# A relu-mean kernel on Trainium2: one store of the results at the end, or two, the larger of them queued behind the loads

## The chip, the cores and the metric

The kernel runs on one core of one Trainium2 chip. The metric is the device time of one execution in microseconds (us). The kernel before takes 161.66 us (median of 6 runs, 161.41 to 161.91). Two executions of the same kernel thus differ by up to 0.5 us.

## The reference

```python
x = np.random.randn(32, 512, 1024).astype(np.float32)      # 67.1 MB
relu_x = np.maximum(x, 0)
return np.mean(relu_x, axis=-1).astype(np.float32)          # (32, 512), 64 KB
```

There are 16384 rows of 1024 numbers, and each gives one result.

## The kernel before

Each of the 128 partitions holds 128 consecutive rows of x, so it makes 128 consecutive results, 512 B of the output. All loads are issued from SP (SyncE) on one queue: seven times 16 rows a partition (the first cut into 1 and 15), then pieces of 8, 4, 2 and 1 rows, and then the last row in three pieces of columns. ACT (ScalarE) and DVE (VectorE) take rows in turn, POOL (GpSimd) scales the sums, and DVE makes the last result (the line called L181 in the profile, the `scalar_tensor_tensor`).

```python
    finish(full, 0, j0)                 # POOL: results 0 to 111 (j0 = 112)
    ...
    finish(i, j0, j0 + lo)              # POOL: results 112 to 125
    ...                                 # POOL: result 126, from two halves, then_inc(pool, 1)
    dve_row(nc, last[:, 512:768], last[:, D + 1:D + 2]).then_inc(dve, 1)
    nc.vector.wait_ge(act, n_done + 1)
    nc.vector.wait_ge(dve, n_done + 1)
    nc.vector.wait_ge(loaded[i + 3], 16)
    nc.vector.scalar_tensor_tensor(     # DVE: result 127
        out=last[:, 768:], in0=last[:, 768:], scalar=0.0, in1=scale[:, :], op0=ALU.max, op1=ALU.mult,
        accum_out=res[:, J - 1:J],
    ).then_inc(dve, 1)

    nc.sync.wait_ge(pool, 2)
    nc.sync.wait_ge(dve, n_done + 2)
    nc.sync.dma_start(out=outr, in_=res[:, :]).then_inc(stored, 16)
    ...
    nc.sync.wait_ge(stored, 16).then_inc(stored, -16)
```

## Time and profile before

| what | value |
|---|---|
| time, median of 6 | 161.66 us |
| span in the profile | 160.3 us |
| DVE, ACT busy | 46%, 43% |
| DMA | 419 GB/s, packets took 97.8% of the span of the 16 transfer engines |
| last load byte, end of the last result, end of the span | 157.55, 158.66, 160.32 us |

The span is 1.3 to 1.4 us shorter than the time. The profile's lines are shown in the prediction. A transfer *lands* when the last of its 16 semaphore writes has arrived (a semaphore is a counter that another engine waits for); *confirmation* is the stretch from the last of these writes' own record to the end of the span. The text below calls *tail* the stretch from the end of the last result (the end of L181's read of the accumulator) to the end of the span: 160.32 - 158.66 = 1.65 us here, by the unrounded figures.

### The profile page before, as it was taken

How to read it: one execution, taken by the hardware profiler on the slowest of the kernel's cores; microseconds unless marked ns; L12 is line 12 of the kernel's file. 1: busy time of each engine (PE TensorE's matmuls, PEld its weight loads, DVE VectorE, ACT ScalarE, POOL GpSimd, SP SyncE). 2: the span in 40 equal slices, each digit the busy share in tenths (PEclk: the TensorE clock that was granted, in tenths of full speed). 3: DMA queues.
4: the chain of work that ended last, by engine and by line, in shares of the span. 5: the costliest groups of instructions: out<-in, count | busy, mean ns of one | idle time of the engine just before them, and what ended most of it. 6: DMA issues, size and time to landing. Idle time of an engine off the chain costs nothing. (4 is left out here: it accounts for less than half of the span.)

```text
span 160.3 us, 344 instructions
## 1 busy us (share of the span) xinstructions
DVE 74.3 (46%) x132; ACT 69.3 (43%) x131; POOL 1.3 (1%) x8
## 2 busy tenths in 40 slices
DVE  0000059700795008940099301991039900498994
ACT  0000059800793008930099101990039700496974
POOL 1000000000000000000000000000000000000001
DMA  9988996996989989979969969969969969999993
GB/s 376 491 383 353 491 523 262 523 523 262 523 360 425 523 360 425 523 327 458 523 294 491 523 278 507 523 262 523 523 262 523 523 262 523 392 392 405 417 404 99
DMA packets 2304, 67.18 MB, mean 419 GB/s; under 512 B 256, under 2 KB 640, under 8 KB 1024
## 3 DMA queue, kind: packets, MB, share of 16 engines
q1 hardware_dynamic: 2304, 67.18, 97.8%
HBM read 67.11 MB, written 0.07 MB: 419 GB/s over the span
## 5 line engine op out<-in xcount | busy, mean ns | idle before, releaser
L20 DVE TENSOR_SCALAR_CACHE_REDUCE rows<-rows 128x1024 f32<-128x1024 f32 x64 | 73.4, 1208 | 84.0 <-DMA rows<-in_x_dram 83.8
L15 ACT ACTIVATE rows<-rows 128x1024 f32<-128x1024 f32 x64 | 66.2, 1036 | 67.0 <-DMA rows<-in_x_dram 66.8
L15 ACT ACTIVATION_READ_ACCUMULATOR rows<-rows 128x1 f32 x64 | 12.0, 187 | 0.0
L15 ACT ACT_TABLE_LOAD x1 | 1.3, 1283 | 21.8 <-DMA rows<-in_x_dram 21.8
L20 DVE DVE_READ_ACCUMULATOR rows<-rows 128x1 f32 x64 | 5.3, 83 | 0.0
L146 POOL TENSOR_SCALAR res<-sums 128x112 f32<-128x112 f32 (+1 forms) x2 | 0.5, 250 | 154.3 <-DVE rows L20 154.3
L15 ACT ACTIVATE last<-last 128x512 f32<-128x512 f32 x1 | 0.6, 629 | 0.0
L20 DVE TENSOR_SCALAR_CACHE_REDUCE last<-last 128x256 f32<-128x256 f32 x1 | 0.4, 420 | 0.3 <-DMA last<-in_x_dram 0.3
L181 DVE SCALAR_TENSOR_TENSOR last<-last,scale 128x258 f32<-128x258 f32 x1 | 0.4, 428 | 0.1
L131 POOL MEMSET scale<- 128x258 f32 x1 | 0.3, 314 | 1.5 <-POOLq L55 1.5
L171 POOL TENSOR_SCALAR res<-part 128x1 f32<-128x1 f32 x1 | 0.3, 264 | 0.6 <-DVE rows L20 0.6
L15 ACT ACTIVATION_READ_ACCUMULATOR last<-last 128x1 f32 x1 | 0.2, 186 | 0.0
L216 POOL MEMSET const-bfloat16-1.0<- 128x1 bf16 x1 | 0.1, 101 | 0.0
L216 POOL MEMSET const-uint8-127<- 128x1 uint8 x1 | 0.1, 101 | 0.0
L216 POOL MEMSET const-float32-0.0<- 128x1 f32 x1 | 0.1, 98 | 0.2 <-issue 0.2
L216 POOL MEMSET const-float32-1.0<- 128x1 f32 x1 | 0.1, 98 | 0.0
L181 DVE DVE_READ_ACCUMULATOR last<-last,scale 128x1 f32 x1 | 0.1, 84 | 0.0
L20 DVE DVE_READ_ACCUMULATOR last<-last 128x1 f32 x1 | 0.1, 83 | 0.0
## 6 DMA issues: line engine op xcount, KB each, us to landing
rows<-in_x_dram SPq DMA_DIRECT2D x1, 7680.0 KB, 21.3
rows<-in_x_dram SPq DMA_DIRECT2D x1, 4096.0 KB, 39.1
rows<-in_x_dram SPq DMA_DIRECT2D x1, 2048.0 KB, 43.6
rows<-in_x_dram SPq DMA_DIRECT2D x2, 512.0 KB, 25.2
rows<-in_x_dram SPq DMA_DIRECT2D x1, 1024.0 KB, 45.7
last<-in_x_dram SPq DMA_DIRECT2D x1, 256.0 KB, 46.7
last<-in_x_dram SPq DMA_DIRECT2D x2, 128.0 KB, 46.5
rows<-in_x_dram SPq DMA_DIRECT2D x6, 48.7
```

The costliest lines, as they stand in the source:

```text
L15: return nc.scalar.activation(out=src, in_=src, func=ACT.Relu, accum_out=acc)
L20: return nc.vector.tensor_scalar(out=src, in0=src, scalar1=0.0, scalar2=init, op0=ALU.max, op1=ALU.add, accum_out=acc,)
L131: nc.gpsimd.memset(scale[:, :], inv).then_inc(pool, 1)
L146: nc.gpsimd.tensor_scalar(out=res[:, lo:hi], in0=sums[:, lo:hi], scalar1=inv, scalar2=0.0, op0=ALU.mult, op1=ALU.add,)
L171: nc.gpsimd.tensor_scalar(out=res[:, J - 2:J - 1], in0=part[:, 0:1], scalar1=part[:, 1:2], scalar2=inv, op0=ALU.add, op1=ALU.mult,).then_i ...
L181: nc.vector.scalar_tensor_tensor(out=last[:, 768:], in0=last[:, 768:], scalar=0.0, in1=scale[:, :], op0=ALU.max, op1=ALU.mult, accum_out=r ...
L216: nc = _bacc.Bacc("TRN2", target_bir_lowering=False, num_devices=1)
```

## The change

112 of the 128 results of a partition are ready at 148 us, 10 us before the last. The change stores these 112 columns in a transfer of their own, queued behind the loads, so that only 16 columns are left for the end.

```diff
             out=res[:, lo:hi], in0=sums[:, lo:hi], scalar1=inv, scalar2=0.0, op0=ALU.mult, op1=ALU.add,
-        )
+        ).then_inc(pool, 1)
 ...
     nc.sync.wait_ge(pool, 2)
+    nc.sync.dma_start(out=outr[:, :j0], in_=res[:, :j0]).then_inc(stored, 16)
     nc.sync.wait_ge(dve, n_done + 2)
-    nc.sync.dma_start(out=outr, in_=res[:, :]).then_inc(stored, 16)
+    nc.sync.wait_ge(pool, 4)
+    nc.sync.dma_start(out=outr[:, j0:], in_=res[:, j0:]).then_inc(stored, 16)
 ...
-    nc.sync.wait_ge(stored, 16).then_inc(stored, -16)
+    nc.sync.wait_ge(stored, 32).then_inc(stored, -32)
```

## The prediction

> **What bounds the kernel now.** I read the page first: the busy shares, then the forty slices.
>
> ```profile
> DVE 74.3 (46%) x132; ACT 69.3 (43%) x131; POOL 1.3 (1%) x8
> ...
> DMA  9988996996989989979969969969969969999993
> GB/s 376 491 383 353 491 523 262 523 523 262 523 360 425 523 360 425 523 327 458 523 294 491 523 278 507 523 262 523 523 262 523 523 262 523 392 392 405 417 404 99
> ...
> HBM read 67.11 MB, written 0.07 MB: 419 GB/s over the span
> ```
>
> No compute engine is busy for half of the span, while the transfer engines are at 90% or so in every slice but the last. 67.11 MB has to come in, and 67.18 MB over 160.3 us is the 419 GB/s shown. So the stream of loads is the bound, and only what lies after it, the tail, can be touched by a change to the store. The queue's own waits and the grouped DMA issues say how the tail is made:
>
> ```profile
> SPq L188 <- DVE last L181: 46.6, 1, 46.6
> SPq L194 <- SPq L194: 1.1, 1, 1.1
> ...
> out_dram<-res SPq DMA_DIRECT2D x1, 64.0 KB, 1.5
> ```
>
> The first line: SP has issued all loads by 112.1 us and then sits 46.6 us for the last instruction on DVE. The second: after the store it waits another 1.1 us for the store's own semaphore. The third: from the start of the issue to landing the one store takes 1.5 us. The timeline of the last microseconds gives the order:
>
> ```profile
> 157.61 0.26 POOL L171 TENSOR_SCALAR res<-part 128x1 f32<-128x1 f32 x1 [0.62 <-DVE rows L20]
> 157.71 0.42 DVE L20 TENSOR_SCALAR_CACHE_REDUCE last<-last 128x256 f32<-128x256 f32 x1 [0.27 <-DMA last<-in_x_dram]
> 157.90 0.19 ACT L15 ACTIVATION_READ_ACCUMULATOR last<-last 128x1 f32 x1
> 158.05 0.08 DVE L20 DVE_READ_ACCUMULATOR last<-last 128x1 f32 x1
> 158.23 0.43 DVE L181 SCALAR_TENSOR_TENSOR last<-last,scale 128x258 f32<-128x258 f32 x1
> 158.58 0.08 DVE L181 DVE_READ_ACCUMULATOR last<-last,scale 128x1 f32 x1
> 158.74 0.35 SPq L189 DMA_DIRECT2D out_dram<-res  x1
> ```
>
> Columns are start, duration, engine and line. The last result exists at 158.66, the store issue starts at 158.74 and takes 0.35 us. A table of stretches splits what follows:
>
> ```profile
> 157.00:157.55 0.55, 0.43 (x2) 0.52 (x3) 0.00 (x0) 1.00 0.46 143
> 157.55:158.74 1.19, 0.86 (x4) 0.54 (x2) 0.26 (x1) 1.00 0.00 0
> 158.74:159.55 0.81, 0.00 (x0) 0.00 (x0) 0.00 (x0) 1.00 0.00 0
> 159.55:159.95 0.40, 0.00 (x0) 0.00 (x0) 0.00 (x0) 1.00 0.57 164
> 159.95:160.30 0.35, 0.00 (x0) 0.00 (x0) 0.00 (x0) 1.00 0.00 0
> ```
>
> The last two columns are the DMA share and GB/s. The loads' last byte moves at about 157.5. The queue is empty until 159.55. The store's bytes move in only 0.40 us, at a share of 0.57, so 0.40 x 0.57 = 0.23 us of work per engine; before them are 0.81 us of issue and start-up, after them 0.35 us of confirmation. Of the 1.5 us of the store, then, only the 0.40 us depends on how many bytes it has.
>
> **What the Trainium skill says.** "DMA: Bandwidth & Descriptors", section "Anatomy of one DMA", splits a transfer into a fixed part, mostly the receipt of the last write, and a part proportional to bytes. It fits that for another issuing path, but the trace agrees in kind: 0.81 + 0.35 us against 0.40 us for 64 KB. "Perfetto Trace Analysis", section "DMA Instruction - HWDGE (DVE, Sync)", says the issue's recorded window ends before the movement, and that the final semaphore write waits for the confirmed write; here 0.35 us of recorded issue and landing 1.15 us after that agree. The first page again, section "Queues, rings and completion order": each engine takes its ring's descriptors in order. So a store issued in mid-stream from the same queue goes behind the loads already there. The trace shows the backlog (loads issued at 110.7 to 111.6 landed 46.4 to 46.7 us later); no store in it shows the order. The section "Specifications" there puts the line-rate minimum at 512 B, with read-modify-write below. The store of before has rows of exactly 128 x 4 = 512 B; the new ones have 448 and 64 B. No run here shows yet what that costs.
>
> **The change, part by part.**
> 1. *Early store.* The POOL multiply for the first 112 columns runs at 147.66 for 0.29 us, thus ends at 147.95 and now signals. With pool at 2 (the fill of the scale tile is 1), SP issues 128 x 448 B = 57 KB at about 148.0, for 0.35 us of SP, which has been waiting since 112. It finds about 157.5 - 148.0 = 9.5 us of loads ahead of it. Its bytes move as each engine runs out of loads, 157.1 to about 157.9, and with 0.35 us of confirmation it lands at about 158.3. That is before SP even issues the second store. On the path: 0.
> 2. *Second store.* It still waits for DVE at 158.66. The fixed parts stay: 0.08 us to the issue, 0.35 us of issue (128 rows as before; the recorded issues of loads, whose sizes differ widely, take 0.33 to 0.44 us, so bytes do not set it), 0.46 us to the first byte, 0.35 us of confirmation. What shrinks is the movement. Each engine still moves 128 / 16 = 8 rows, of 64 B in place of 512 B. From 0.23 us / 8 = about 28 ns a row of 512 B, I estimate 10 to 15 ns for a row of 64 B, as a row has a fixed part; 8 of them are about 0.1 us. So 0.23 - 0.1 = **0.13 us saved**. The rest of the 0.40 us is that engines do not start together, which stays.
> 3. *Extra wait.* Before, the wait for pool came ahead of the wait for DVE and was long satisfied. Now a wait for pool (4, reached near 157.87) comes after the DVE wait, on the path. DVE passes its three waits ahead of L181 in 158.23 - 158.13 = 0.10 us, thus about 0.03 us each: **0.03 us added**, if SP is like DVE.
> 4. *Signals and end wait.* Two more POOL increments and a final wait for 32 in place of 16: POOL is 1% busy, and the end wait is set by the second store. 0.
>
> Sum: -0.13 + 0.03 = **-0.10 us**, 0.06% of the time. 161.68 - 0.10 = 161.58, which I round to **161.6 us**.
>
> **Rivals.**
> *A. Short rows cost more.* If writing 64 B into a 512 B row takes a read first, the second store's movement or confirmation grows. A read and a write more would cost around the 0.35 us that confirmation takes now (an estimate). [...] For it: the skill's threshold. The time would be 161.68 + 0.03 + 0.2 to 0.35 = about 161.9 to 162.1, so slower by 0.1 to 0.2%.
> *B. The early store delays the last loads.* The load of the last columns was issued at about 111.58 and landed 46.4 us later, 157.98. L181 started at 158.23, when ACT (158.09) and DVE (158.13) had been done; I put the load's slack at 0.15 us. Engines that finish their loads early would send the store while late ones still read. The whole store is 0.23 us of work per engine, and ring order puts it behind on each single engine, so at most 0.1 us would show: 161.7. If it were not queued behind but mixed in, the stream itself would lengthen by its 0.2 us: 161.8.
> *C. The bytes were all that counted.* Were the 1.5 us proportional to bytes, an eighth of them would leave 0.2 us and the time would be 160.4. The empty stretches before and after the movement speak against it. Even so it is 0.8%, within 2%.
> *D. Nothing at all.* If the movement's 0.40 us is wholly spread between engines, the gain is 0 and the extra wait costs 0.03: 161.7.
>
> **Range and chances.** The mechanism lies within about -0.15 to +0.4 us. The three runs of before span 161.49 to 161.85, thus 0.36 us, which is more than the expected effect; the stream of loads, where 1% is 1.6 us, can also differ from one chip or session to another. I take 161.2 to 162.0, three quarters of it noise. For 2% the time would have to move 3.2 us; the whole tail after the last load byte is 160.3 - 157.5 = 2.8 us, and the store only 1.5 of it. So faster by over 2% is excluded short of an error in reading (0.01); slower by over 2% would need the early store to block the stream for 3 us (0.01); within 2% is 0.98.
>
> **What would show it right or wrong.** Right: two stores among the issues, the first of 56 KB issued near 148 with some 10 us to landing, the second of 8 KB issued within 0.2 us of L181's end with about 1.4 us to landing; its movement under 0.40 us; loads' last byte still near 157.5; L181 still near 158.2. A second store landing in 1.6 us or more is rival A; a later L181 after a later load is rival B; 0.5 us to landing is rival C. The prediction is wrong outright if the early store is issued well after 148, if the time per load changes, or if the gap between L181 and the second issue grows by more than 0.1 us.

## The result, and the profile after

The changed kernel takes 161.53 us (median of 6 runs, 161.43 to 161.74) against 161.66 us. The ratio is 0.9994 with a 95% interval of 0.9981 to 1.0006, so the two are the same at 2%, and this measurement alone does not tell the difference from none. Ratios here are the mean time of one kernel's fast runs over that of the other's of the same rounds, so they are not quite the ratio of the medians quoted.

The single profiles show what the times cannot. The DMA issues of the changed kernel (KB and us to landing), and the queue's own waits:

```profile
out_dram<-res SPq DMA_DIRECT2D x1, 56.0 KB, 10.2
out_dram<-res SPq DMA_DIRECT2D x1, 8.0 KB, 1.4
...
SPq L189 <- POOL res L146: 35.9, 1, 35.9
SPq L191 <- POOL res L171: 9.5, 1, 9.5
SPq L197 <- SPq L197: 1.0, 1, 1.0
SPq L192 <- DVE last L181: 0.8, 1, 0.8
```

The early store waits 10.2 us in the queue and lands; the late one takes 1.4 us in place of 1.5. The wait for DVE is now put down to L192, the store itself, where before it was L188, a line ahead of the store. That turns out to matter. The timeline's end:

```profile
147.96 0.35 SPq L189 DMA_DIRECT2D out_dram<-res  x1
...
158.01 0.08 DVE L20 DVE_READ_ACCUMULATOR last<-last 128x1 f32 x1
158.18 0.43 DVE L181 SCALAR_TENSOR_TENSOR last<-last,scale 128x258 f32<-128x258 f32 x1
158.54 0.08 DVE L181 DVE_READ_ACCUMULATOR last<-last,scale 128x1 f32 x1
158.65 0.34 SPq L192 DMA_DIRECT2D out_dram<-res  x1
```

The last result exists at 158.62 and the issue starts at 158.65, 0.03 us later; before, it was 0.08 us. The stretches of the tail (the last two columns are the DMA share and GB/s):

```profile
157.70:158.65 0.95, 0.83 (x4) 0.35 (x2) 0.13 (x1) 1.00 0.00 0
158.65:159.48 0.83, 0.00 (x0) 0.00 (x0) 0.00 (x0) 1.00 0.00 0
159.48:159.70 0.22, 0.00 (x0) 0.00 (x0) 0.00 (x0) 1.00 0.42 38
159.70:160.10 0.40, 0.00 (x0) 0.00 (x0) 0.00 (x0) 1.00 0.00 0
```

Issue and start-up are as long as before (0.83 against 0.81 us with these borders), the movement is about half as long (0.22 against 0.40 us), the confirmation is as long. The trace's records of single packets give the same without rounding to borders:

| part of the tail, us | before | after |
|---|---|---|
| end of the last result to start of the issue | 0.08 | 0.03 |
| start of the issue to the first row's start | 0.85 | 0.84 |
| first row's start to the end of the last semaphore write | 0.36 | 0.21 |
| from there to the end of the span | 0.38 | 0.39 |
| sum | 1.65 | 1.47 |
| mean time of one row on its engine, ns | 27.2 (512 B) | 10.4 (64 B) |

(The columns are rounded one by one.) So the tail is 0.18 us shorter, 0.19 by the unrounded figures: 0.15 of it from the movement, 0.05 from the issue, less 0.01 in a longer confirmation. The loads end at the same time (157.55 and 157.50 us).

### The profile page after: what moved, and what is told of

It reads as the page before. It is cut to its first block, busy times and chain, and to the rows that moved or that the text cites. A ratio compares the mean times of both kernels' runs of the same rounds, so it can differ in the third digit from the quotient of the medians.

```text
span 160.1 us, 345 instructions
## 1 busy us (share of the span) xinstructions
DVE 74.3 (46%) x132; ACT 69.3 (43%) x131; POOL 1.3 (1%) x8
## 5 line engine op out<-in xcount | busy, mean ns | idle before, releaser
L181 DVE SCALAR_TENSOR_TENSOR last<-last,scale 128x258 f32<-128x258 f32 x1 | 0.4, 428 | 0.1
L181 DVE DVE_READ_ACCUMULATOR last<-last,scale 128x1 f32 x1 | 0.1, 83 | 0.0
```

Source lines behind the costliest of these rows:

```text
L181: nc.vector.scalar_tensor_tensor(out=last[:, 768:], in0=last[:, 768:], scalar=0.0, in1=scale[:, :], op0=ALU.max, op1=ALU.mult, accum_out=r ...
```

## The experiments

Three questions: is the 0.18 us real and made as the table says; does the wait's place explain the 0.05 us; and is the early store free?

### The changed kernel again

No edit.

> The changed kernel once more, for an interval and a second profile. My theory: the tail from L181's end to the end of the span is 1.47 us in the changed kernel's profile against 1.65 us before, made of 0.05 us less to the issue and 0.15 us less of movement; so 0.1 to 0.2 us less time, a ratio of 0.9988 to 0.9994. Rival (the shorter tail of one profile is chance): the tail of this profile lies at 1.6 us or more, or the ratio is centred on 1.000.

161.47 us (median of 5) against 161.70; ratio 0.9984, interval 0.9971 to 0.9997. The second profile has nearly the same tail: 0.03 + 0.84 + 0.21 + 0.40 = 1.48 us. The theory stands and the rival falls. The ratio this time excludes 1 by a little, and its centre, 0.26 us, is more than the 0.18 us of the tail; the first ratio's centre was 0.10 us. Both intervals hold 0.18 us.

### Where the wait sits

The order in which two waits are written decides which of them the store carries. In the built program the first one written is carried by the store itself and the later one becomes a semaphore instruction of its own ahead of it. The kernel before wrote POOL first, so the wait that ends last, for DVE, sat in the separate instruction, and the store had to follow it. The change wrote DVE first for its second store. The waits in the profiles show it: the one for DVE is put down to the line of the store or to a line ahead of it.

```diff
 # before_swap, against the kernel before
-    nc.sync.wait_ge(pool, 2)
     nc.sync.wait_ge(dve, n_done + 2)
+    nc.sync.wait_ge(pool, 2)
     nc.sync.dma_start(out=outr, in_=res[:, :]).then_inc(stored, 16)
 # after_swap, against the changed kernel
-    nc.sync.wait_ge(dve, n_done + 2)
     nc.sync.wait_ge(pool, 4)
+    nc.sync.wait_ge(dve, n_done + 2)
     nc.sync.dma_start(out=outr[:, j0:], in_=res[:, j0:]).then_inc(stored, 16)
```

> The kernel before with the waits ahead of its one store written in the other order, DVE first and POOL second. In the built program the wait written first is carried by the store itself and the other becomes an instruction of its own ahead of it. Theory of the wait's place: the gap from L181's end to the start of the issue falls from 0.08 to about 0.03 us, all else stays, the movement stays 0.35 to 0.40 us; 0.05 us less time, within the noise. Rival (the gap of 0.08 was chance, or belongs to the size of the store): the gap stays at 0.08 us.

> The changed kernel with the waits ahead of the second store in the other order, POOL first and DVE second. Theory of the wait's place: the gap rises from 0.03 to about 0.08 us while the movement of 64 B rows stays at about 0.2 us; the tail after L181 is about 1.52 us. Rival (the gap belongs to the second store's shape, or the early store has woken the queue): the gap stays at 0.03 us.

The wait for DVE and the timeline's end of the kernel before with its waits swapped (L189 is the store):

```profile
SPq L189 <- DVE last L181: 0.8, 1, 0.8
...
158.73 0.09 DVE L181 DVE_READ_ACCUMULATOR last<-last,scale 128x1 f32 x1
158.84 0.35 SPq L189 DMA_DIRECT2D out_dram<-res  x1
```

and of the changed kernel with its waits swapped (L192 is the store):

```profile
SPq L191 <- DVE last L181: 10.4, 1, 10.4
...
158.81 0.08 DVE L181 DVE_READ_ACCUMULATOR last<-last,scale 128x1 f32 x1
158.97 0.34 SPq L192 DMA_DIRECT2D out_dram<-res  x1
```

The gap follows the order of the waits and not the store: 0.03 us with the large store (158.840 - 158.812 before rounding), 158.97 - 158.89 = 0.08 us with the small one. The trace also records the separate instruction, which the views leave out: in the kernel before and in after_swap it starts 0.028 us after the last result and takes 0.017 us, and the store starts 0.030 us after its end; where the store carries the wait, it starts 0.028 us after the last result. The movement keeps its length (0.36 and 0.21 us). The tails are 1.60 and 1.52 us. The rivals fall. The times do not resolve it: 161.66 us, ratio 0.9999 (0.9986 to 1.0012), and 161.54 us, ratio 0.9990 (0.9978 to 1.0003).

### Two stores, neither early

```diff
-    nc.sync.wait_ge(pool, 2)
-    nc.sync.dma_start(out=outr[:, :j0], in_=res[:, :j0]).then_inc(stored, 16)
     nc.sync.wait_ge(dve, n_done + 2)
     nc.sync.wait_ge(pool, 4)
+    nc.sync.dma_start(out=outr[:, :j0], in_=res[:, :j0]).then_inc(stored, 16)
     nc.sync.dma_start(out=outr[:, j0:], in_=res[:, j0:]).then_inc(stored, 16)
```

> The changed kernel with its first store moved behind the DVE wait, so both are issued at the end, one after the other. Theory (the gain is the early start of the first store, and an issue on SP costs 0.35 us): the second issue starts 0.35 us later than in the changed kernel and ends the span, about 0.37 us later than there: tail about 1.85 us after L181, time about 0.2 us above the kernel before. Rival (the two stores overlap, and splitting costs nothing even at the end): tail within 0.1 us of that of the kernel before, 1.65 us.

The end of its timeline:

```profile
158.98 0.08 DVE L181 DVE_READ_ACCUMULATOR last<-last,scale 128x1 f32 x1
159.09 0.35 SPq L190 DMA_DIRECT2D out_dram<-res  x1
159.48 0.43 SPq L191 DMA_DIRECT2D out_dram<-res  x1
```

The second issue starts 0.39 us after the first and takes 0.43 us in place of 0.34. The tail is 1.95 us, 0.10 more than expected, and the time is 162.05 us, ratio 1.0020 (1.0007 to 1.0033). The rival falls: at the end of the kernel a second store costs 0.30 us more than one store (0.35 against before_swap, whose store also carries the wait for DVE). What the change gains, it gains from the early issue.

### The size of a late row

```diff
 # half: 64 columns early, 64 late
-    nc.sync.dma_start(out=outr[:, :j0], in_=res[:, :j0]).then_inc(stored, 16)
+    nc.sync.dma_start(out=outr[:, :64], in_=res[:, :64]).then_inc(stored, 16)
 ...
-    nc.sync.dma_start(out=outr[:, j0:], in_=res[:, j0:]).then_inc(stored, 16)
+    nc.sync.dma_start(out=outr[:, 64:], in_=res[:, 64:]).then_inc(stored, 16)
 # split126: 126 columns early (after the second POOL multiply), 2 late
-    nc.sync.wait_ge(pool, 2)
-    nc.sync.dma_start(out=outr[:, :j0], in_=res[:, :j0]).then_inc(stored, 16)
+    nc.sync.wait_ge(pool, 3)
+    nc.sync.dma_start(out=outr[:, :J - 2], in_=res[:, :J - 2]).then_inc(stored, 16)
 ...
-    nc.sync.dma_start(out=outr[:, j0:], in_=res[:, j0:]).then_inc(stored, 16)
+    nc.sync.dma_start(out=outr[:, J - 2:], in_=res[:, J - 2:]).then_inc(stored, 16)
```

> Split at column 64 in place of 112: the late store has 128 rows of 256 B. Theory (a row's time on its engine is a fixed part and a part by bytes, from 27.2 ns at 512 B and 10.4 ns at 64 B): about 17.6 ns a row, a movement window of about 0.26 us, all fixed parts of the tail as in the changed kernel (0.84 us from issue to first byte, 0.39 us from last byte to the end). Rival A (rows under 512 B need a read first): more than 27 ns a row, or confirmation longer than 0.39 us.

> Split at column 126: the late store has 128 rows of 8 B, and the early store waits for the second POOL multiply (about 157.0). Theory: 8 ns or so a row, the window 0.02 us shorter than in the changed kernel, tail 1.45 us; the early store lands near 158.5, ahead of the second. Rival A in its strong form (8 B pieces must be read, merged and written): the late store's landing grows from 1.4 us to 1.6 us or more.

| late rows | ns a row | first row to last semaphore write, us | from there to the end, us | tail, us |
|---|---|---|---|---|
| 512 B (before) | 27.2 | 0.36 | 0.38 | 1.65 |
| 256 B (half) | 17.6 | 0.26 | 0.38 | 1.51 |
| 64 B (after) | 10.4 | 0.21 | 0.39 | 1.47 |
| 8 B (split126) | 8.5 | 0.20 | 0.40 | 1.47 |

A row costs about 8 ns and 0.0375 ns a byte, the slope being (27.2 - 10.4) / (512 - 64). The rival of short rows falls for these stores: none of the four sizes breaks the line, and confirmation stays within 0.38 to 0.40 us. From 64 B down to 8 B the tail no longer falls. In split126 the early store, issued only at 157.30, landed at 158.84 (158.5 expected), and the tail is 1.47 us (1.45 expected).

### Without the early store

```diff
-    nc.sync.wait_ge(pool, 2)
-    nc.sync.dma_start(out=outr[:, :j0], in_=res[:, :j0]).then_inc(stored, 16)
 ...
-    nc.sync.wait_ge(stored, 32).then_inc(stored, -32)
+    nc.sync.wait_ge(stored, 16).then_inc(stored, -16)
```

The result is wrong, as 112 columns are never written.

> The changed kernel without its early store: the first 112 columns are never written, so the result is wrong on purpose. Theory (early store is free): tail after L181 and the time are those of the changed kernel, within 0.05 us in the profile. Rival B: the last loads land sooner by up to 0.1 us and the second store's start-up is shorter than 0.84 us.

The tail is 1.49 us, against 1.47. From the last load byte to the complete semaphore of that load it takes 0.47 us, and it takes 0.44 before, 0.47 and 0.39 in the two profiles of the changed kernel. 161.46 us (median of 4), ratio 0.9981 (0.9955 to 1.0007). So one early store of 448 B rows costs nothing that shows.

### A heavier early store

To see whether the early store is free because it lies behind the loads, or only because it is small, it was cut into eight stores of 14 columns each, 1024 rows in all.

```diff
-    nc.sync.dma_start(out=outr[:, :j0], in_=res[:, :j0]).then_inc(stored, 16)
+    for q in range(0, j0, 14):
+        nc.sync.dma_start(out=outr[:, q:q + 14], in_=res[:, q:q + 14]).then_inc(stored, 16)
 ...
-    nc.sync.wait_ge(stored, 32).then_inc(stored, -32)
+    nc.sync.wait_ge(stored, 144).then_inc(stored, -144)
```

> The early store cut into eight of 14 columns (56 B rows), all issued near 148: 1024 rows, so 64 rows and 8 semaphore writes per engine, by 10 ns about 0.7 us of work per engine where one early store takes 0.2. Theory (behind the loads, off the path): the last loads land and L181 starts at the same time after the last load byte as before, the early stores land by about 158.8, the end of the span moves by less than 0.1 us. Rival B (early store delays the loads): L181 starts about 0.5 us later, or the loads' last pieces land that much later relative to the last big load.

The first theory failed. Rival B's forecast of a late L181 came true, but not by the bytes. The timeline before its last result (in brackets: idle time and what ended it):

```profile
157.75 0.08 DVE L20 DVE_READ_ACCUMULATOR last<-last 128x1 f32 x1
158.34 0.43 DVE L181 SCALAR_TENSOR_TENSOR last<-last,scale 128x258 f32<-128x258 f32 x1 [0.51 <-DMA last<-in_x_dram]
```

The loads' bytes were not delayed: the last one, at 157.21, came 45.85 us after the issue of the last load, against 45.88 in the changed kernel. But the last load's semaphore was complete only at 158.22, 1.00 us after its last byte. DVE sat idle 0.51 us for it, where in the changed kernel L181 waits for DVE's and ACT's last results and this load is in before them. The stores' semaphore writes came between 157.54 and 159.75, where 158.8 was expected for the last. The eight issues also kept SP for 6.67 us, not eight times 0.35; SP then waited for DVE until 158.80, so this cost nothing here. The time is 161.98 us (median of 4, 161.38 to 162.53), ratio 1.0024 (0.9984 to 1.0064). As this was one profile, the same kernel ran again, and beside it one with the same rows in a single store: its results lie in SBUF in 8 groups of 14 with gaps, so that they cannot be joined.

```diff
 # early_rows, against the changed kernel (that finish() takes the two patterns is left out)
+    apart = sbuf("apart", P, 8, 16)
 ...
-    finish(full, 0, j0)
+    finish(full, 0, j0, apart[:, :, :14], sums[:, :j0].rearrange("p (q c) -> p q c", q=8))
 ...
-    nc.sync.dma_start(out=outr[:, :j0], in_=res[:, :j0]).then_inc(stored, 16)
+    nc.sync.dma_start(out=outr[:, :j0].rearrange("p (q c) -> p q c", q=8), in_=apart[:, :, :14]).then_inc(stored, 16)
```

> The kernel with eight early stores once more. In its first profile the last load's bytes ended at 157.21 but its semaphore was complete only at 158.22, 1.00 us later (0.44 and 0.47 us in the kernel before and the changed one), and DVE sat idle 0.51 us for that load ahead of L181. Theory (packets queued behind a load hold up the confirmation of its landing, though not its bytes): again 0.8 us or more from last byte to landing, and an idle stretch of DVE ahead of L181. Rival (chance of one execution): 0.5 us or less, no idle stretch.

> One early store of the same 1024 rows of 56 B: the first 112 results lie in SBUF in 8 groups of 14 with gaps, so one issue and one semaphore write per engine in place of eight, and about the same rows. Theory 1 (the many rows behind the load hold up its landing): last byte to landing of the last load 0.8 us or more, L181 late. Theory 2 (the eight semaphore writes, each of which waits for the data ahead of it, hold it up): 0.5 us or less, L181 0.09 us after DVE's last read, and the time that of the changed kernel.

Eight stores again: 0.98 us from last byte to landing, 0.52 us idle, 161.92 us, ratio 1.0016 (0.9993 to 1.0038). It is no chance. One store of these rows is worse: 1.92 us to landing, and 163.15 us, ratio 1.0085 (1.0066 to 1.0104). The waits of its DVE (in all, times, longest, us; L182 is the last result in this file):

```profile
DVE last L182 <- DMA last<-in_x_dram: 1.5, 1, 1.5
```

So it is not the number of semaphore writes but the rows. They differ from the changed kernel's in two ways: there are eight times as many, and they are 56 B long, so that most begin off a multiple of 64 B. The last kernel has 7 groups of 16 columns, 896 rows of 64 B, all at multiples of 64 B.

```diff
 # early_rows64, against early_rows
-    apart = sbuf("apart", P, 8, 16)
+    apart = sbuf("apart", P, 7, 24)
 ...
-    finish(full, 0, j0, apart[:, :, :14], sums[:, :j0].rearrange("p (q c) -> p q c", q=8))
+    finish(full, 0, j0, apart[:, :, :16], sums[:, :j0].rearrange("p (q c) -> p q c", q=7))
 ...
-    nc.sync.dma_start(out=outr[:, :j0].rearrange("p (q c) -> p q c", q=8), in_=apart[:, :, :14]).then_inc(stored, 16)
+    nc.sync.dma_start(out=outr[:, :j0].rearrange("p (q c) -> p q c", q=7), in_=apart[:, :, :16]).then_inc(stored, 16)
```

> One early store again in many short rows, now 7 groups of 16 columns: 896 rows of 64 B, each at a multiple of 64 B in the output, 56 per engine. With 1024 rows of 56 B the last load's landing came 1.92 us after its last byte and the time rose to 163.15 us. Theory of number (rows queued behind the load hold up its confirmation): again 1.2 us or more from last byte to landing, DVE idle for it ahead of L181, time at 162.4 us or more. Theory of alignment (rows that begin and end off a multiple of 64 B are slow to write, and that holds it up): 0.5 us from last byte to landing, the time that of the changed kernel, 161.5 us.

```profile
158.34 0.08 DVE L20 DVE_READ_ACCUMULATOR last<-last 128x1 f32 x1
158.52 0.43 DVE L182 SCALAR_TENSOR_TENSOR last<-last,scale 128x258 f32<-128x258 f32 x1
```

In its timeline the idle stretch is gone. Last byte to landing is 0.47 us, as in the changed kernel, and the time is 161.73 us, ratio 0.9991 (0.9967 to 1.0016). Number falls as the cause (56 rows an engine here, 64 there), alignment stands. The length of a row and its place went together here: rows of 56 B that all begin at multiples of 64 B did not run.

| early store | rows of an engine | last load byte to that load's landing, us | last load byte to the early store's last landing, us | time, us |
|---|---|---|---|---|
| none (no_early) | 0 | 0.47 | - | 161.46 |
| one, 448 B rows (after) | 8 | 0.47 | 0.67 | 161.53 |
| one, 64 B rows (early_rows64) | 56 | 0.47 | 1.07 | 161.73 |
| eight, 56 B rows (early_eight) | 64 | 1.00 | 2.53 | 161.98 |
| one, 56 B rows (early_rows) | 64 | 1.92 | 3.08 | 163.15 |

What stays open is whether a row off a multiple of 64 B is slow by itself, or only where two neighbouring rows written close together share a block of 64 B. The 126-column split speaks for the second: its 504 B and 8 B rows are off such multiples, only 8 to an engine, and they landed in 1.5 and 1.4 us. In early_rows the store landed 2.62 us after its last row; less the usual 0.4, that is some 0.035 us for each of an engine's 64 rows (an estimate), and 8 such rows would have added some 0.3 us. That much does not show, but one number of rows is no proof. How writes behind a load hold up that load's semaphore is not shown either.

### A try at a better version

L181 too has waits of which one is carried. In the changed kernel it carries the wait for ACT; here it carries the one for DVE's own last result, which comes last.

```diff
-    nc.vector.wait_ge(act, n_done + 1)
     nc.vector.wait_ge(dve, n_done + 1)
+    nc.vector.wait_ge(act, n_done + 1)
     nc.vector.wait_ge(loaded[i + 3], 16)
```

> The changed kernel with the waits ahead of L181 reordered so that L181 itself carries the wait for DVE's own last result, which comes last (158.09), and the instruction ahead of it those for ACT and the load. Theory of the wait's place: the gap from DVE's read of the accumulator to L181 falls from 0.08 or 0.09 us to about 0.03, the tail after L181 stays at 1.47 us; some 0.05 us less than the changed kernel, about 161.45, which is inside the noise of the times. Rival (DVE waits for its own write to be confirmed, and that is the gap): the gap stays at 0.08 us or more.

```profile
158.09 0.19 ACT L15 ACTIVATION_READ_ACCUMULATOR last<-last 128x1 f32 x1
158.21 0.08 DVE L20 DVE_READ_ACCUMULATOR last<-last 128x1 f32 x1
158.36 0.43 DVE L181 SCALAR_TENSOR_TENSOR last<-last,scale 128x258 f32<-128x258 f32 x1
```

The gap is 158.36 - 158.29 = 0.07 us, not 0.03; in the changed kernel it is 158.18 - 158.09 = 0.09 us. The trace's record of the separate instruction says why: ACT ended at 158.271, 0.02 us before DVE (158.294), its wait is now in that instruction, which ended at 158.315, and L181 started 0.046 us after that end. In the changed kernel L181 starts 0.045 us after the same instruction's end. So the wait for ACT set the start here, the rival is not needed, and what carrying the last wait is worth on DVE stays unmeasured. 161.39 us (median of 6), ratio to the kernel before 0.9977 (0.9962 to 0.9992). That is the lowest median of all. The interval lies below 1, by far less than 2%; whether it beats the changed kernel is not resolved, since the intervals overlap.

## Why the prediction was right

The predicted time, 161.6 us, held, and the range of 161.2 to 162.0 holds every one of the six runs. That tests little: rivals B and D, and no effect at all, would have stayed inside the range too. (The drift between chips or sessions that the range allowed for did not show: the kernel before had medians of 161.66 to 161.70 us throughout.) What tests the prediction are the parts of the tail. By its steps:

- **The bound and the tail.** Right, but one line was misread: the DMA row is not at 90% or so in every slice but the last, as eight of the other 39 show 60 or 70%. What carries the bound is that packets took 97.8% of the engines' span. The loads' stream is untouched (420 against 419 GB/s), and all that changed lies in the tail.
- **Step 1, the early store.** Right: issued at 147.96 (148.0 predicted), landed 10.2 us later at 158.17 (158.3 predicted), at no cost on the path.
- **Step 2, the movement.** Right in mechanism, and nearly in size: 0.15 us saved in place of 0.13, a row of 64 B takes 10.4 ns (10 to 15 estimated). The fixed parts stayed: 0.84 us to the first row, 0.34 us of it issue, and 0.39 us of confirmation. "DMA: Bandwidth & Descriptors" in the Trainium skill, section "Anatomy of one DMA", which the prediction cites for a fixed part, puts most of it in the receipt of the last write, on another issuing path; here more of it lies ahead of the bytes (0.84 us) than after them (0.39). Also, landing comes 1.20 us after the recorded end of the issue before, not 1.15, which came from the rounded 1.5.
- **Step 3, the extra wait.** Wrong in sign. I added 0.03 us for a wait that "comes after the DVE wait, on the path". In the built program the wait written second goes ahead as an instruction of its own, and the store carries the first. So the change took an instruction off the path, and 0.05 us came off. Both swaps show it. The 0.03 us itself was from a false count: ahead of L181 there is one separate instruction with two waits, and L181 carries the third.
- **The sum.** -0.10 us was predicted for the tail; -0.18 us is what the profiles show: 0.03 + 0.05 + 0.02 more, from the two steps above, less 0.02 of rounding and confirmation. The time's first ratio, -0.10 us at its centre, does not decide between them, as its interval is 0.4 us wide. That it meets the predicted -0.10 is luck: the second ratio's centre is -0.26 us.
- **Rivals.** A fell for rows of 256, 64 and 8 B. C fell: 1.4 us to landing, not 0.2. D fell: the movement did shrink. B did not happen in the change, but it lies close by in a form I had not thought of: an early store delays the *landing* of the last load, not its bytes, if its rows are many and lie off multiples of 64 B.

## What to carry to other kernels

Issuing a store early behind a queue of loads hides it well, but what a late store then saves is only its bytes' movement, here 0.15 us of 1.5; issue, start-up and confirmation were paid at every size tried, and a second store issued at the end cost more than it saved. Write the wait that will end last so that the store itself carries it (0.05 us here, in the profiles alone), and look at the profile's waits for which line that is, as source order may mislead. And if a store behind loads is cut into many short rows, try them at multiples of 64 B: 1024 rows of 56 B, though off the path, held up the semaphore of the load ahead of them and cost some nine times what the split gained (163.15 - 161.53 = 1.6 us against 0.18).

## What the Trainium skill lacked or had wrong

- "DMA: Bandwidth & Descriptors", section "Specifications", has read-modify-write below 512 B. No cost of that shows for late rows of 256, 64 and 8 B: 17.6, 10.4 and 8.5 ns a row, and a landing 1.4 us after the issue in the last two. What did cost, short rows written off multiples of 64 B, is not on the page: 1024 rows of 56 B, most of them off such multiples (time 163.15 us), against 896 rows of 64 B at such multiples (161.73 us).
- The same page, section "Queues, rings and completion order", says that a semaphore write lands after earlier writes of its engine. It does not say that writes queued behind a load can delay that load's landing: 1.92 us after its last byte in place of 0.47.
- The same page, section "Latency and other measured facts", gives about 600 ns to the first byte for a transfer issued from SP. It does not say from when. In all late stores here that were issued alone it is 0.83 to 0.85 us from the start of the issue to the first row, and 0.49 to 0.50 us from the issue's recorded end.
- "Perfetto Trace Analysis", section "Identifying Dependency Chains", says that an instruction with several waits may get semaphore instructions put ahead of it. It does not say which wait goes where, nor the price: 0.08 us from the last result to the issue where the last-ending wait sits in the separate instruction, 0.03 us where the store carries it.
